# First output weights in a sixteen-place ring, and four kinds of load tied behind others, in a decoder trunk on one core

## The chip, the cores and the metric

The kernel runs on one core of one Trainium2 chip. The metric is the time of one execution in microseconds (us) of device time; lower is better. The engines are named as in the profile: PE is TensorE's matmul, PEld its weight load, DVE is VectorE, ACT is ScalarE, POOL is GpSimd, SP is SyncE. SP computes nothing here: it issues most of the DMA transfers, in its own program order, one after the other. A name with a q (SPq, ACTq) is that engine's sequencer, which issues DMAs. L1343 is line 1343 of the kernel before.

## The reference

One layer of a hybrid decoder (sequence 1024, model width 2048): two groups of eight heads, a projection of both, a gated embedding, two norms.

```python
hn = rmsnorm(h, norm_mix_g)
sb_q, sb_k, sb_v, sb_g, df_q, df_k, df_v, df_g = split(hn @ w_in)      # 2048 x 8192
sb_out = stick_breaking_attention(sb_q, sb_k, sb_v)                    # 8 heads of 128
df_out = differential_attention(rope(df_q), rope(df_k), df_v, lam)     # 8 heads, 2 x 64
df_out = rmsnorm(df_out, subln_g, 1e-5) * (1 - lambda_init)
mixed  = concat(sb_out * silu(sb_g), df_out * silu(df_g))
h = h + mixed @ w_out                                                  # 2048 x 2048
gate = sigmoid(rmsnorm(h, norm_ple_g) @ w_ple_gate)                    # 2048 x 2048
h = h + gate * (p @ w_ple_proj)                                        # 256 x 2048
return rmsnorm(h, norm_final_g)
```

All of it is float32.

## The kernel before

**Numbers.** Each float32 operand is split into a high and a low part (`hi`: a cast on ACT, `lo`: a subtraction on DVE), and a product is three matmuls, hi.hi, hi.lo and lo.hi. So each weight tile and each operand tile passes ACT and then DVE before PE can use it.

**Products by halves.** The sequence is cut into two halves of 512 columns. The three large products (value and gate columns of `w_in`; `w_out`; `w_ple_gate`) multiply 2 x 2 blocks with seven products instead of eight (`class Seven`). The seven are called A11, A12, S1, S2, S3, S4, A22; their operands are blocks or sums of blocks, kept in DRAM (`mixed_d`, `comb_d`, `h_d`, `hcomb_d`) and loaded back into SBUF (`load_operand`, `gate_operand`).

**Stages, in order of time.** Values and gates of all heads (to about 640 us), q and k projections with attention for the second half and then for the first half (`for half in (1, 0)`, 16 heads each, to about 1700 us), the output projection (`w_out`, to about 1980 us), the gate products with `w_ple_gate` (to about 2310 us), the end with the final norm.

**The first output products.** The products A11 and A12 of all eight units `u` of `w_out` (phase 0) run while the last head's attention still runs. Their split weights were made earlier and lie in DRAM (`wout_d[u, k, i]`: k is A11 or A12, i is hi or lo). `last_steps` hands their loads to `side`, a list of steps that are called after so many ticks; a tick is three matmuls of the main sequence. The last q/k unit is ticks 0 to 32, then come sixteen products of four ticks each in the order A11(0), A11(1), A12(0), A12(1), A11(2) and so on: A11(3) begins at tick 52. `weights_first(u, ...)` (L1338) loads two tiles of 512 KB for one u: one holds hi of A11 and of A12, the other lo of both. The tiles come from the places named by tag: `wraw`, `whi`, `wlo`, `st`, two places each. Unit 0 and unit 3 both take the two `wraw` places.

**Who sets the order.** The order on PE, ACT and DVE is that in which the code is written (`manual_schedule`). SP's and POOL's order is made by a scheduler with a simulated clock: a DMA is issued when, by that clock, its place and its data are free, however much later in the code it stands. On the chip SP then goes through that order strictly, and waits at each DMA until its place is really free. `tc.issue_after(x)` adds one condition to the scheduler: not ahead of x on that queue.

**The gate products.** `op.todo` lists the weight tiles in the order of use. `step()` is called after each half product (a slot: twelve matmuls): it casts the next weight tile on ACT (`whigh`, L758), subtracts on DVE (`wlow`, L772), calls what is due, and takes up to two entries from `xq`, which are splits of operands (L644 on ACT, L650 on DVE). Loads of the raw gate weights are `first_load` (L1545, for A11 and A12: `w_gate`), `second_load`, and `last_load` (L1563, for S3 and A22: from `tw_d`). `first_load` reuses one place for each product and half, so the load for unit u+1 waits until DVE is done with that of unit u. Only unit 7's A12 has a place of its own (`awl`).

`gate_loads` (L1266) calls `gate_operand` (L1250), which issues the DMA, and puts the split into `xq` to be taken `GLAT` slots later (3 for A11 and A12, 4 for S1, S2, S4, 2 for the others).

**The last pass** (second part of the gate stage: S3 and A22 of units 0 to 5, then 6 and 7 by column halves) needs for each unit u the residual tile `hpair[u]` (512 KB, `load_h`, L1982) for the addition at L2038, and for the second half's final scaling sixteen tiles `h_d[1, ch]` (256 KB, `final1`). Before, `load_h` is called for 0 to 3 ahead of the pass and for u+4 in unit u.

Of the kernel before, what the change touches and what calls it, by code (L numbers as in the profile page):

```python
# [13 lines left out]
F32 = mybir.dt.float32  # L14
F32R = mybir.dt.float32r
# [5 lines left out]
P = 128  # L21
# [14 lines left out]

PRIO = 300
GVT = 1, 2, 3, 4, 5, 6, 7, 8, 14, 15, 16, 17
GLAT = {'S4': 4, 'S1': 4, 'S2': 4}
TICK = {  # L40
    "sumlag": 2, "gvx": ((22, 27), (80, 85)), "chore": (36, 78, 87), "opx": (8, 12), "turn": 76, "lag": 15, "gap": (4, 6),
    "parts": (1, 2), "vparts": (3, 4), "sums": (0, 2), "squared": (3, 4.5), "norm": (1, 4),
# [9 lines left out]
    "begun": (86.5, 91.5, 93.5, 94.5, 93.5), "mid_turn": 76, "mid_lag": 17, "mid_gap": (4, 6),  # L52
    "mid_df_scores": (-20, -16, -9, -8.5, -1, -0.5, 4, 8), "mid_df_turn": (19, 17), "mid_df_v": -1, "mid_df_norm": 44.5,
    "mid_sb_scores": (-3, 5, 12.5, 21), "mid_sb_turn": (32, 36), "mid_sb_v": 22, "mid_taken": (28, 31),
# [15 lines left out]
def _body(ctx, nc, tc, ap):  # L70
# [3 lines left out]
    wp = ctx.enter_context(tc.tile_pool(name="wp", bufs=2))  # L74
# [174 lines left out]
    wout_d = dram.tile([8, 2, 2, P, HALF], F32R, name="wout_d", tag="wout_d")  # L249
# [30 lines left out]
    h_d = dram.tile([2, NK, P, HALF], F32, name="h_d", tag="h_d")  # L280
# [312 lines left out]
    with tc.tile_pool(name="at", bufs=2) as at, tc.tile_pool(name="pz", bufs=2, space=PSUM) as pz:  # L593
        SWAP = [i + 8 if i < 8 else i - 8 if i < 16 else i for i in range(32)]
        BUFS = {"cs": 1, "bt": 3}
# [498 lines left out]
        for ph in range(2):  # L1094
            for u in range(NVG):
# [3 lines left out]
                if ph:  # L1099
                    a = pp.tile([P, HALF], F32, name="pa", tag="acc", bufs=2)  # L1100
# [120 lines left out]


        op = Seven(lambda u, ph, k: ap["w_out"][u, ph, k], 8)
        tw_d = dram.tile([8, 2, P, 2, HALF], F32, name="tw_d", tag="tw_d")
        hcomb_d = dram.tile([4, 8, P, HALF], F32, name="hcomb_d", tag="hcomb_d")
        q_d = dram.tile([8, 2, P, HALF], F32, name="q_d", tag="q_d")
# [23 lines left out]
        def gate_operand(nm, i, eng):  # L1250

            hi, lo = op.places(GPLACE[nm][i], "g" + nm)
            src = {"A11": h_d[1, i], "A12": h_d[1, i + 8], "A22": h_d[0, i + 8]}.get(nm)
            if src is None:
                src = hcomb_d[SUMS.index(nm), i]
            gain = {"A11": i, "A12": i + 8, "A22": i + 8, "S3": i}.get(nm)
            if gain is not None:
                gain = gvec[:, 1, gain:gain + 1]
            if nm == "S3":
                with tc.issue_after(op.lastw.ins):  # L1260
                    eng.dma_start(lo.bitcast(F32), src)
            else:
                eng.dma_start(lo.bitcast(F32), src)
            return partial(op.split, "g" + nm, i, hi, lo, gain, apart=True)

        def gate_loads(nm, i0, n=4, eng=nc.sync):  # L1266
# [15 lines left out]
        kept, place = [], [0]  # L1282
# [52 lines left out]
                    side.add([(lag, load_operand(0, nm, i))])  # L1335
                side.add([(t0, load)])

        def weights_first(u, t0, pool, tags):  # L1338

            def load():  # L1340
                hl = [pool.tile([P, 2, 4 * P], F32R, name=f"wf{nm}", tag=t, bufs=2) for nm, t in zip(("hi", "lo"), tags)]
                for i in range(2):
                    nc.sync.dma_start(hl[i].bitcast(F32), wout_d[u, :, i].bitcast(F32).rearrange("k p n -> p k n"))  # L1343
                for k, nm in enumerate(("A11", "A12")):
                    op.wq[u, 0, nm] = hl[0][:, k], hl[1][:, k]

            side.add([(t0, load)])

        def last_steps():
            for nm in ("A11", "A12", "S2", "S4", "S1", "S3", "A22"):  # L1350
                operands(nm, *TICK[nm])
            raws, high = (wp, "wraw", "wraw"), (wp, "whi", "wlo")
            for u, (pool, *tags) in enumerate((raws, high, high, raws, high, high, (at, "st", "st"), high)):
                weights_first(u, TICK["wf"][u], pool, tags)
            side.add(zip(TICK["begun"], (begun, op.whigh, led, led, led)))

        def begun():
# [8 lines left out]
        cs = rope_of(1)  # L1366
# [4 lines left out]
        for half in (1, 0):  # L1371
            X = X0 if half == 0 else X1

            for hd in ORDER:
# [110 lines left out]
                q, k, qz, KL = qk[0], qk[1], qk.get("qz"), qk.get("kl")  # L1485
# [18 lines left out]
                if half == 1 and hd == ORDER[-2]:  # L1504
                    cs = rope_of(0)
# [32 lines left out]
        def wg(u, ks, b):  # L1538
            return ap["w_gate"][u, ks, b // 10 - 1][:, b % 10 - 1, :]

        raws = {}
# [3 lines left out]
        def first_load(u, nm, ks):  # L1545

            if u < 8:
                if u == 7 and nm == "A12":
                    t = at.tile([P, 4 * P], F32, name="wraw1", tag="awl")
                else:  # L1550
                    if (u, ks) == (0, 0):
                        first[nm] = wp.tile([P, 2, 4 * P], F32, name="wraw", tag="wraw", bufs=2)
                    t = first[nm][:, ks, :]
                raws.setdefault((u, nm), []).append(t)
                nc.sync.dma_start(t, wg(u, ks, 11 if nm == "A11" else 21))
            if ks and (u == 7 and nm == "A12" or u == 8 and nm == "A11"):
                first.pop(nm)
                w = wp.tile([P, 2, 4 * P], F32, name="wraw", tag="wraw", bufs=2)
                for i, b in enumerate((22, 21) if u == 7 else (12, 11)):
                    raws[0, 1, b] = w[:, i, :]  # L1560
                    second_load(0, 1, b)

        def last_load(u, nm):  # L1563
            if u < 8:
                w = wp.tile([P, 2, 4 * P], F32, name="wraw", tag="wraw", bufs=2)
                raws[u, nm] = [w[:, ks, :] for ks in range(2)]
                nc.sync.dma_start(w, tw_d[u, int(nm == "A22")])

        def second_load(u, ks, b):
            nc.sync.dma_start(raws[u % 2, ks, b], wg(u, ks, b))  # L1570
# [411 lines left out]
        def load_h(u):  # L1982
            if u < 8:
                hpair[u] = at.tile([P, 2, HALF], F32, name="h0", tag=HP[u], bufs=BUFS.get(HP[u], 2))
                nc.sync.dma_start(hpair[u], h_d[0].rearrange("(a k) p t -> k p a t", a=2)[u])

        def load_q(u):

# [6 lines left out]
        embedding(0)  # L1995
        plew(0, 1, "awl")
        plew(0, 0)
        for u in range(4):
            load_h(u)
        qs = {u: load_q(u) for u in range(3)}  # L2000
        s2 = ev.tile([P, HALF], F32, name="s2", tag="ssq")
# [14 lines left out]

        def final1(ch, u_):
            t = ftile()
            nc.sync.dma_start(t, h_d[1, ch])

            def fn():
                V.scalar_tensor_tensor(t, t, gvec[:, 2, ch:ch + 1], sums1[0], op0=ALU.mult, op1=ALU.mult)
                nc.sync.dma_start(out_f[ch * P:ch * P + P, Q:], t)

            if u_ < 5:
                op.soon.append((op.slot + 3, fn))
            else:
                late.append(fn)
# [44 lines left out]
        for u in range(6):  # L2073
            embedded = begin(u + 1) if u < 5 else None
            if u == 5:
                for c in (1, 0):
                    plew_load(7, c)
            gprod(u, "A22", bs[u], False)
            q1, _ = qs.pop(u)
            V.tensor_tensor(q1, bs[u], q1, op=ALU.add)  # L2080
            gating0(u, 0, q1, zs[u])
            if embedded:
                embedded()
            if u < 5:
                qs[u + 3] = load_q(u + 3)
            load_h(u + 4)
            if u == 0:
                sums1 = load_sums(1, ((ev, "rstd1", 1), (ev, "sq", 2)))
            elif u == 1:
                norm(sums1)  # L2090
            else:
                for ch in range(4 * u - 8, 4 * u - 4):
                    final1(ch, u)
# [265 lines left out]
```

## Time and profile before

| | |
|---|---|
| median of 3 runs | 2345.38 us (2342.2 to 2348.5) |
| profiled execution | 2351.75 us, span 2350.0 us |
| PE busy | 2315.6 us of the span (99%), 11089 matmuls |
| PEld, DVE, ACT, POOL busy | 82%, 76%, 54%, 13% |
| granted TensorE clock, mean | 0.996 |
| DMA | 556.66 MB, mean 237 GB/s |

The span runs from the first to the last instruction; the profiled execution's own time is 1.75 us more. Matmuls are pipelined: the record of a 128x512 one is about 0.39 us long, but in a full sequence one starts every 0.23 us, so the times that count are the starts. The idle time ahead of a matmul stands in brackets in the timeline, with what ended it.

### The profile page before, as it was taken

How to read it: one execution, taken by the hardware profiler on the slowest of the kernel's cores; microseconds unless marked ns; L12 is line 12 of the kernel's file. 1: busy time of each engine (PE TensorE's matmuls, PEld its weight loads, DVE VectorE, ACT ScalarE, POOL GpSimd, SP SyncE). 2: the span in 40 equal slices, each digit the busy share in tenths (PEclk: the TensorE clock that was granted, in tenths of full speed). 3: DMA queues.
4: the chain of work that ended last, by engine and by line, in shares of the span. 5: the costliest groups of instructions: out<-in, count | busy, mean ns of one | idle time of the engine just before them, and what ended most of it. 6: DMA issues, size and time to landing. Idle time of an engine off the chain costs nothing. (4 is left out here: it accounts for less than half of the span.)

```text
span 2350.0 us, 32639 instructions
## 1 busy us (share of the span) xinstructions
PE 2315.6 (99%) x11089; PEld 1931.3 (82%) x11089; DVE 1797.0 (76%) x3119; ACT 1268.5 (54%) x2303; POOL 296.2 (13%) x441
## 2 busy tenths in 40 slices
PE   9999999999999999999999999999899999999998
PEld 7878888888788888877888888888778887888777
DVE  7487776666578888877877878778677988687787
ACT  6323243333357776677766767677633435542455
POOL 2121111111100000000011010111021121111000
PEclk9999999999999999999999999999999999999999
DMA  8586788866787777787677667678798789998965
GB/s 268 204 293 229 254 276 229 209 157 131 210 266 258 238 252 258 254 288 253 199 201 203 181 198 216 194 206 255 221 246 203 248 245 286 308 349 258 336 210 185
DMA packets 255000, 556.66 MB, mean 237 GB/s; under 512 B 28512, under 2 KB 39008, under 8 KB 254832
## 3 DMA queue, kind: packets, MB, share of 16 engines
q1 hardware_dynamic: 185424, 395.92, 50.9%
q0 software_dynamic: 52848, 128.74, 22.5%
q10 hardware_dynamic: 16560, 29.92, 3.5%
q8 instruction: 87, 1.43, 0.2%
q14 instruction: 81, 0.66, 0.1%
HBM read 359.16 MB, written 203.69 MB: 240 GB/s over the span
## 5 line engine op out<-in xcount | busy, mean ns | idle before, releaser
L758 ACT CAST wpr<-T 128x512 fp32r<-128x512 f32 x208 | 127.1, 621 | 484.1 <-DVE T L717 406.4
L267 PE MATMUL acc<-xh,whi 128*128 128x512 f32 x768 | 313.1, 408 | 0.2 <-ACT whi L185 0.2
L269 PE MATMUL acc<-xh,wlo 128*128 128x512 f32 x768 | 301.6, 393 | 4.4 <-DMA wlo<-wlo_d 3.9
L268 PE MATMUL acc<-xl,whi 128*128 128x512 f32 x768 | 300.9, 392 | 0.0
L269 PEld LDWEIGHTS acc<-xh,wlo 128*128 128x128 f32 x768 | 144.4, 188 | 37.4 <-DMA wlo<-wlo_d 4.3
L267 PEld LDWEIGHTS acc<-xh,whi 128*128 128x128 f32 x768 | 144.9, 189 | 25.1 <-ACT whi L185 0.6
L268 PEld LDWEIGHTS acc<-xl,whi 128*128 128x128 f32 x768 | 145.1, 189 | 23.8 <-issue 0.2
L772 DVE TENSOR_TENSOR wpr<-T,wpr 128x512 fp32r<-128x512 f32 x208 | 142.4, 684 | 6.1 <-ACT wpr L758 3.0
L871 POOL DMA_DIRECT2D vg_d<-hc x128 | 89.1, 696 | 453.9 <-DVE hc L1089 263.1
L185 ACT CAST whi<-wraw 128x1024 fp32r<-128x1024 f32 x128 | 134.1, 1048 | 19.0 <-DMA wraw<-w_in 8.8
L758 ACT CAST wpr<-wraw 128x512 fp32r<-128x512 f32 x128 | 78.8, 617 | 106.3 <-DMA wraw<-tw_d 38.1
L406 ACT ACTIVATE et<-z,mx 128x512 f32<-128x512 f32 (+7 forms) x128 | 95.1, 743 | 60.6 <-DVE mx L398 60.6
L398 DVE CUSTOM_DVE_ANT_0 z<-z,wide 128x512 f32<-128x512 f32 (+7 forms) x128 | 97.5, 763 | 33.3 <-PE z L351 30.4
L477 DVE TENSOR_TENSOR awl<-tp,awh 128x256 fp32r<-128x256 f32 (+1 forms) x160 | 92.5, 578 | 34.9 <-ACT awh L472 33.9
L472 ACT CAST awh<-tp 128x256 fp32r<-128x256 f32 (+1 forms) x160 | 80.6, 504 | 51.4 <-PE tp L453 50.5
L772 DVE TENSOR_TENSOR wpr<-wraw,wpr 128x512 fp32r<-128x512 f32 x128 | 86.6, 684 | 17.2 <-ACT wpr L758 17.1
L381 DVE TENSOR_TENSOR_SCAN pt<-pt 128x511 f32<-128x511 f32 (+3 forms) x64 | 86.7, 1354 | 14.4 <-ACT pt L374 13.9
L181 DVE TENSOR_TENSOR wlo<-wraw,whi 128x1024 fp32r<-128x1024 f32 x56 | 68.5, 1223 | 15.3 <-ACT whi L185 14.8
L500 PE MATMUL av<-awl,v 128*128 128x256 f32 x256 | 72.9, 285 | 0.4 <-DVE awl L477 0.4
L498 PE MATMUL av<-awh,v 128*128 128x256 f32 x256 | 72.5, 283 | 0.5 <-ACT awh L472 0.4
L499 PE MATMUL av<-awh,v 128*128 128x256 f32 x256 | 72.4, 283 | 0.0
L413 ACT ACTIVATE et<-et,l 128x512 f32<-128x512 f32 (+3 forms) x64 | 49.4, 772 | 40.9 <-DVE l L412 40.9
(580 smaller groups left out, 6917.6 us busy)
## 6 DMA issues: line engine op xcount, KB each, us to landing
wraw<-w_in SPq DMA_DIRECT2D x128, 512.0 KB, 4.7
wlo<-wlo_d SPq DMA_DIRECT2D x72, 512.0 KB, 3.8
wraw<-w_vg SPq DMA_DIRECT2D x143, 256.0 KB, 3.6
vg_d<-hc POOLq DMA_DIRECT2D x128, 256.0 KB, 4.9
wlo_d<-wlo SPq DMA_DIRECT2D x56, 512.0 KB, 3.7
wraw<-w_gate SPq DMA_DIRECT2D x92, 256.0 KB, 5.3
h_d<-hc POOLq DMA_DIRECT2D x56, 256.0 KB, 5.1
wraw<-w_out SPq DMA_DIRECT2D x56, 256.0 KB, 4.5
```

The source lines that it names most:

```text
L185: side.later(1, lambda: A.copy(hi[:, o], raw[:, o]))
L267: T.matmul(acc[c], hi[:, k2, kh, c, :], xh, start=first, stop=False)
L268: T.matmul(acc[c], hi[:, k2, kh, c, :], xl, start=False, stop=False)
L269: T.matmul(acc[c], lo[:, k2, kh, c, :], xh, start=False, stop=last)
L381: V.tensor_tensor_scan(pt[:, w], pt[:, w], pt[:, w], initial=1.0, op0=ALU.mult, op1=ALU.bypass)
L398: V.tensor_tensor_reduce(z[:, vw], z[:, vw], add, -DF_SCALE, 3.0e38, ALU.add, ALU.min, mx)
L406: A.activation(et[:, vw], z[:, vw], AF.Exp, bias=mx[:, 0:1], scale=-1.0, accum_out=l[:, c:c + 1])
L472: A.copy(wh[:, o, :], tp[:, o, :])
L477: V.tensor_tensor(wl[:, o, :], tp[:, o, :], wh[:, o, :].bitcast(F32), op=ALU.subtract)
L758: A.copy(t[:, 0], src)
L772: V.tensor_tensor(t[:, 1], src, t[:, 0].bitcast(F32), op=ALU.subtract)
L871: G.dma_start(vg_d[hf, blk, u], o, **(dict(accum_op=ALU.add) if ph else {}))
```

## The change

Five edits.

1. `weights_first` loads one tile for each product (u, k), with hi and lo of that product, in one DMA of 512 KB; sixteen DMAs, as before. The tiles go round a longer ring: `wraw`, `wraw`, `cs`, `whi`, `wlo`, `whi`, `wlo`, twice, and `st` for the last two. The times of the requests are sixteen instead of eight.
2. The DMAs of the gate operands A12, blocks 0 to 3, are issued after the last `first_load` that stands ahead of them in the code (`op.lastf`).
3. The gate weights A12 of unit 7 are issued after the last of the other `first_load`s (`op.lastf`).
4. `load_h` is called for units 0 and 1 ahead of the last pass, behind the load of gate operand A22 block 3 (`op.lasta[0]`), and for u+2 in unit u, behind the last `tw_d` load (`op.lastl`). The loads of `final1` also go behind `op.lastl`.
5. The splits of the gate operands S3 are taken one slot later (`GLAT` 3 instead of 2).

```diff
-GLAT = {'S4': 4, 'S1': 4, 'S2': 4}
+GLAT = {'S4': 4, 'S1': 4, 'S2': 4, 'S3': 3}
...
-    "wf": (21.5, 25, 33, 45, 49, 61, 65.5, 77),
+    "wf": (18, 21.5, 22, 25, 25.5, 33, 33.5, 38, 42, 46, 50, 54, 58, 62, 66, 70),
...
-            if nm == "S3":
-                with tc.issue_after(op.lastw.ins):
+            if nm == "S3" or nm == "A12" and i < 4:
+                with tc.issue_after((op.lastw if nm == "S3" else op.lastf).ins):
                     eng.dma_start(lo.bitcast(F32), src)
             else:
-                eng.dma_start(lo.bitcast(F32), src)
+                op.lasta[i // 4] = eng.dma_start(lo.bitcast(F32), src)
...
-        def weights_first(u, t0, pool, tags):
+        def weights_first(u, k, t0, pool, tag):
             def load():
-                hl = [pool.tile([P, 2, 4 * P], F32R, name=f"wf{nm}", tag=t, bufs=2) for nm, t in zip(("hi", "lo"), tags)]
-                for i in range(2):
-                    nc.sync.dma_start(hl[i].bitcast(F32), wout_d[u, :, i].bitcast(F32).rearrange("k p n -> p k n"))
-                for k, nm in enumerate(("A11", "A12")):
-                    op.wq[u, 0, nm] = hl[0][:, k], hl[1][:, k]
+                t = pool.tile([P, 2, 4 * P], F32R, name="wfhl", tag=tag, bufs=BUFS.get(tag, 2))
+                nc.sync.dma_start(t.bitcast(F32), wout_d[u, k].bitcast(F32).rearrange("i p n -> p i n"))
+                op.wq[u, 0, ("A11", "A12")[k]] = t[:, 0], t[:, 1]
...
-            raws, high = (wp, "wraw", "wraw"), (wp, "whi", "wlo")
-            for u, (pool, *tags) in enumerate((raws, high, high, raws, high, high, (at, "st", "st"), high)):
-                weights_first(u, TICK["wf"][u], pool, tags)
+            raw, high, low, st, cs_ = (wp, "wraw"), (wp, "whi"), (wp, "wlo"), (at, "st"), (at, "cs")
+            ring = raw, raw, cs_, high, low, high, low, raw, raw, cs_, high, low, high, low, st, st
+            first_of = [(u + i, k) for u in range(0, 8, 2) for k in range(2) for i in range(2)]
+            for (u, k), t0, place in zip(first_of, TICK["wf"], ring):
+                weights_first(u, k, t0, *place)
...
-                nc.sync.dma_start(t, wg(u, ks, 11 if nm == "A11" else 21))
+                if u == 7 and nm == "A12":
+                    with tc.issue_after(op.lastf.ins):
+                        nc.sync.dma_start(t, wg(u, ks, 21))
+                else:
+                    op.lastf = nc.sync.dma_start(t, wg(u, ks, 11 if nm == "A11" else 21))
...
-                nc.sync.dma_start(w, tw_d[u, int(nm == "A22")])
+                op.lastl = nc.sync.dma_start(w, tw_d[u, int(nm == "A22")])
...
-                nc.sync.dma_start(hpair[u], h_d[0].rearrange("(a k) p t -> k p a t", a=2)[u])
+                with tc.issue_after((op.lasta[0] if u < 2 else op.lastl).ins):
+                    nc.sync.dma_start(hpair[u], h_d[0].rearrange("(a k) p t -> k p a t", a=2)[u])
...
-        for u in range(4):
+        for u in range(2):
             load_h(u)
...
-            nc.sync.dma_start(t, h_d[1, ch])
+            with tc.issue_after(op.lastl.ins):
+                nc.sync.dma_start(t, h_d[1, ch])
...
-            load_h(u + 4)
+            load_h(u + 2)
```

More of the change, by code (lines that the diff above doesn't have):

```diff
@@ L1223, in _body @@
         op = Seven(lambda u, ph, k: ap["w_out"][u, ph, k], 8)
+        op.lasta = [None, None]
         tw_d = dram.tile([8, 2, P, 2, HALF], F32, name="tw_d", tag="tw_d")
```

2 rows, old and new, of the table TICK are left out of this document.

## The prediction, made before the changed kernel was run

> **What bounds the kernel now.** I read the profile in this order: busy time by engine, the waits of PE, the timeline of PE around its longest waits, the timeline of SP for the DMAs behind them, and a table of stretches for clock, DMA and DVE.
>
> ```profile
> PE 2315.6 (99%) x11089; PEld 1931.3 (82%) x11089; DVE 1797.0 (76%) x3119; ACT 1268.5 (54%) x2303; POOL 296.2 (13%) x441
> PE pa L665 <- DMA wflo<-wout_d: 3.0, 1, 3.0
> PE pa L663 <- DMA wfhi<-wout_d: 2.3, 1, 2.3
> PE pa L1790 <- ACT s L1856: 1.9, 1, 1.9
> PE pb L1790 <- DVE qt L2080: 1.2, 1, 1.2
> PE pb L1790 <- DVE qt L2057: 1.1, 1, 1.1
> PE z L1703 <- DVE pl L1681: 0.5, 1, 0.5
> PE z L1704 <- DVE pwhl L1695: 0.4, 1, 0.4
> ```
>
> PE is busy for 99% of the span, and the change takes no matmul away. So it can only win PE's waits, and what a wait costs after it. The columns of the waits are the sum in us, how often, and the longest. The first two are one place, a first output product that waits for its weights. The third is the start of the gate stage. The last four lie in the last pass: 1.2 + 1.1 + 0.5 + 0.4 = 3.2 us.
>
> **The change part by part.**
>
> *The ring of the first output weights.* The timeline of PE around the first two waits (start, record length, instruction, idle time ahead of it):
>
> ```profile
> 1642.50 0.39 PE L663 MATMUL pa<-cA11h,wfhi 128*128 128x512 f32 x1
> 1645.72 0.39 PE L664 MATMUL pa<-cA11l,wfhi 128*128 128x512 f32 x1
> 1646.64 0.40 PE L665 MATMUL pa<-cA11h,wflo 128*128 128x512 f32 x1
> 1649.37 0.47 PE L663 MATMUL pa<-cA11h,wfhi 128*128 128x512 f32 x1 [2.33 <-DMA wfhi<-wout_d]
> 1653.07 0.79 PE L665 MATMUL pa<-cA11h,wflo 128*128 128x512 f32 x1 [3.00 <-DMA wflo<-wout_d]
> 1658.55 0.40 PE L664 MATMUL pa<-cA11l,wfhi 128*128 128x512 f32 x1
> ```
>
> 1642.50 is the first matmul of A11 of unit 2, 1649.37 that of unit 3. It should have started 0.23 us after 1646.64, at 1646.87. From the first matmul of a product to the second of its second block (L664), with the attention's matmuls between, unit 2 took 1645.72 - 1642.50 = 3.22 us. Unit 3 has one short attention matmul more between (0.12 us), so it would have come to 1646.87 + 3.34 = 1650.21, and came at 1658.55: 8.3 us lost. Of that 5.3 us is idle time; the other 3.0 us is slow running after it, which the stretches show (length, busy us with instruction counts of PE, PEld, DVE, ACT, POOL, granted clock, DMA share, GB/s):
>
> ```profile
> 1630.00:1640.00 10.00, 10.00 (x56) 8.61 (x55) 9.31 (x18) 6.87 (x14) 3.10 (x4) 1.00 0.84 294
> 1640.00:1650.00 10.00, 7.67 (x40) 5.89 (x37) 7.01 (x16) 5.40 (x12) 1.74 (x3) 1.00 1.08 262
> 1650.00:1660.00 10.00, 7.00 (x27) 6.00 (x27) 2.20 (x6) 1.46 (x4) 0.00 (x0) 0.66 0.89 287
> ```
>
> The granted clock falls to 0.66 in the ten microseconds after the wait began: the wait is followed by half speed. The Trainium skill, page "TensorE: Matmul & The Clock Gate", Part 1, has PE drop to half rate after about one idle window of 3.4 us and return after one busy window of that length. By that page one window at half rate would cost 1.7 us (an estimate), and this place 5.3 + 1.7 = 7.0 us instead of 8.3. The trace has 3.0 us, and I go by the trace.
>
> Why the weights were late:
>
> ```profile
> 1639.03 0.86 SPq L1343 DMA_DIRECT2D wfhi<-wout_d  x1
> 1639.98 1.56 SPq L1343 DMA_DIRECT2D wflo<-wout_d  x1
> DMA to landing us min/median/max: 4.5/5.7/13.0
> ```
>
> Unit 3 takes both `wraw` places of unit 0, and they are free when A12 of unit 0 ends (tick 44). SP issues at 1639.03 and 1639.98, and the second lands about 13 us later, the longest of the eight, with the DMA engines full (1.08). It was needed eight ticks after the place was free.
>
> In the new ring I go through all sixteen places. A11 of unit 3 is in `whi`, whose place is free when the last q/k unit ends (tick 32), and is needed at tick 52. From the eighth tile on, each takes the place of a product six or more places before: `wraw` is free at ticks 36 and 40 for products at 60 and 64, `cs` at 44 for 68, `whi` and `wlo` at 48 to 60 for 72 to 84. All have 20 ticks or more from a free place to the need. From 1625 on, where the last unit ends, a tick is more than a microsecond (eight ticks took from about 1639 to 1647), so 20 ticks are over 20 us, against 13.0 us for the slowest landing. The first three come in places that are free inside the last unit. Bytes and number of DMAs stay the same (sixteen of 512 KB). The price of the wait, 8.3 us, should go.
>
> What is late next: DVE. It was busy for 9.31 of 10 us just ahead of the wait and only 2.20 in the ten after, so the wait gave it time to catch up; without it the attention's steps follow more closely. PE ran with that DVE load without a stop from 1630 to 1640, so I charge only 0.8 us, between 0 and 4 us (half the prize).
>
> SP gets other waits in its order: each new load waits for the end of one product instead of two. What stands behind it can be late by at most one product, four ticks, some 4 us, and the loads behind (operands of the next products, `w_out` blocks) are needed tens of ticks later. The two `w_out` blocks that go into the second `wraw` place start up to 4 ticks later, for a cast at tick 91.5. I cost that at nothing; the cover is the 23 ticks between.
>
> *A12 operands and unit 7's gate weights.* Start of the gate stage, SP and ACT:
>
> ```profile
> 1953.95 1.03 SPq L1555 DMA_DIRECT2D wraw<-w_gate  x2
> 1956.62 3.26 SPq L1555 DMA_DIRECT2D wraw<-w_gate  x4
> 1965.05 2.95 SPq L1263 DMA_DIRECT2D cgA12l<-h_d  x4
> 1968.34 0.33 SPq L1555 DMA_DIRECT2D wraw<-w_gate  x1
> 1971.06 0.62 ACT L758 CAST wpr<-wraw 128x512 fp32r<-128x512 f32 x1 [1.30 <-DMA wraw<-w_gate]
> 1976.85 0.62 ACT L758 CAST wpr<-wraw 128x512 fp32r<-128x512 f32 x1 [1.75 <-DMA wraw<-w_gate]
> 1981.30 0.63 ACT L1289 ACTIVATE rsq<-hc 128x512 f32<-128x512 f32 x1 [1.56 <-DMA sq_d<-rsq]
> ```
>
> Two and four `w_gate` loads go out ahead of any cast. Units 0 and 1 share four places, so six must hold the two of unit 7, which are not cast until 28 weight tiles later. The change sends them away. The four A12 operands of 1965.05 (1 MB) move behind the second load of unit 1's A11, which is the one of 1968.34: it lands with 1 MB less ahead of it, and ACT's 1.75 us at 1976.85 should shrink. Whether PE's 1.9 us goes depends on the wait at 1981.30, since between it and the copy that PE waits for ACT has no pause. That is a DMA of squares in the same full queues. The operands themselves now land later, about 1976 to 1979 by 6 to 8 us from 1969 to 1971, and ACT takes the first two at 1977.9 or sooner. So the gain lies between 1.9 us and a loss of about 1 us. I take 1.2.
>
> *The last pass.*
>
> ```profile
> 2205.00:2210.00 5.00, 5.00 (x22) 3.72 (x20) 4.96 (x9) 2.97 (x6) 0.00 (x0) 1.00 1.06 392
> 2260.00:2280.00 20.00, 20.00 (x90) 16.57 (x89) 15.45 (x26) 11.81 (x20) 0.00 (x0) 1.00 0.36 119
> 2197.87 3.11 SPq L1985 DMA_DIRECT2D h<-h_d  x4
> 2205.83 0.40 SPq L1567 DMA_DIRECT2D wraw<-tw_d  x1
> 2211.59 1.97 SPq L1985 DMA_DIRECT2D h<-h_d  x4
> h<-h_d SPq DMA_DIRECT2D x8, 512.0 KB, 10.1
> wraw<-tw_d SPq DMA_DIRECT2D x16, 512.0 KB, 3.9
> 2214.34 0.62 ACT L758 CAST wpr<-wraw 128x512 fp32r<-128x512 f32 x1 [6.37 <-DMA wraw<-tw_d]
> 2217.27 0.39 PE L1790 MATMUL pb<-cgS3h,wpr 128*128 128x512 f32 x1
> 2230.30 0.72 ACT L644 ACTIVATE cgA22h<-cgA22l,gvec 128x512 fp32r<-128x512 f32 x1 [1.61 <-DMA cgA22l<-h_d]
> 2242.29 0.38 SPq L1567 DMA_DIRECT2D wraw<-tw_d  x1
> 2260.38 0.69 DVE L2038 TENSOR_TENSOR h<-h,qt 128x512 f32<-128x512 f32 x1
> ```
>
> All eight residual tiles (4 MB) go out at 2197.87 to 2213.6, in the stretch where the DMA engines are full (1.06). The weights issued at 2205.83 land 8.5 us later instead of their median 3.9, and ACT waits 6.37 us for them; A22's operands are late too. From there the lateness goes through ACT and DVE to PE's four waits. The change moves six of the eight tiles (3 MB, some 8 us of DMA time at 392 GB/s) past 2240, into a stretch where the share falls to 0.36. PE's 3.2 us is the most that can be won. I take 2.8.
>
> Are they in time? The tile of unit 2 goes behind the `tw_d` load of 2242.29 and is first used by the addition at 2260.38: 18 us, against 10.1 us for the landing in the full queues. Each later one has the same distance, one unit, some 13 us after the last. The loads of `final1` are used three slots after they are asked for; they leave the full stretch too.
>
> The later S3 splits frame a small risk: the last pair now stands behind the cast of 2214.34 on ACT. The row leaves 2.9 us (2214.34 to 2217.27, where PE starts S3) for cast, norm and split, too little if that weight tile lands as late as before. With the residual tiles gone it should land about 4 us sooner. Between 0 and 3 us; I take 0.
>
> *Sum.* 8.3 - 0.8 + 1.2 + 2.8 = 11.5 us. Against the profiled execution's own 2351.75 us (span 2350.0 and 1.75 around it) that is 2340.2 us. The median of the runs shown is 2345.38, 6.4 us below the profiled one, and I take the same gain from it: 2333.9 us.
>
> **The rivals.**
>
> *Only the ring wins.* The gate stage and the last pass keep their waits, or the S3 splits give back what the residual tiles win: 8.3 - 0.8 = 7.5 us, 2337.9 us. For it: the 1.9 us hangs on the squares' DMA, which no edit moves. Against it: the full DMA share exactly where the loads are taken out.
>
> *The ring's prize is given back.* The attention of the last head is bound by DVE, so that PE waits in small pieces for what it waited for in one: half of 8.3 and all other gains gone, 4 us, 2341.4 us. For it: 9.31 of 10 us. Against it: no stop of PE in that stretch. That a load is simply not asked earlier is excluded by the places in the code.
>
> *The residual tiles come late (slower).* Each is now behind a weight load that itself waits for DVE, and DVE's addition holds up all behind it on DVE, the additions that free PE's accumulators too. The margin is 18 - 10 = 8 us. If a tile lands later than 18 us after its turn, DVE stands in each of six units. To be slower by 0.3% (7 us) this must take back 11.5 + 7 us, about 3 us a unit: landings 21 us after the turn, twice the 10.1. Then 2353 us. The Trainium skill, page "DMA: Bandwidth & Descriptors", section on rules for kernel authors, speaks for this rival: issue a DMA early and wait on it late. The trace's rows speak against it here, since early is when the queues were full.
>
> *More than forecast.* A late weight tile costs this at the start of the output stage:
>
> ```profile
> 1731.84 0.50 PE L663 MATMUL pbc<-cS2h,wpr 128*128 128x512 f32 x1 [1.21 <-ACT wpr L758]
> ```
>
> If SP's new order happens to bring that tile's load forward, the 1.21 us and a spell at half clock like the one above (3 us) go as well: 2329.7 us.
>
> **How the numbers follow.** About 0.3%, 7 us, is what a measurement of this kernel can tell from no change. Forecast 0.46; only the ring 0.21; given back 0.14; slower 0.10; more 0.09. Faster by over 7 us (below 2338.3): forecast, more, and half of the ring's case, whose 2337.9 is at the bound: 0.66. Same: the other half and the given-back case less a little: 0.22. Slower: 0.12, the residual tiles and unforeseen waits from SP's reordering. The predicted time is 2333.9. The range goes down to 2328 (the case of more, with 2 us of run spread) and up to 2347 (the given-back case with its spread, up to the time before).
>
> **What would show it.** Right: no wait of PE on a load from `wout_d`, and a granted clock of 1.00 between 1640 and 1660; a `tw_d` landing near 4 us and no ACT wait above 3 us around 2205; residual loads spread past 2240; PE's third wait below 1 us. Wrong: DVE additions at L2038 waiting for `h<-h_d`, PE waits for attention tiles after 1640, or new waits on `w_out` blocks behind SP.

## The result, and the profile after

The changed kernel takes 2334.32 us (median of 4 runs, 2332.48 to 2337.18), the kernel before, run beside it, 2346.34 us: a ratio of 0.9952, 95% interval 0.9933 to 0.9971, so 12.0 us less. A second comparison (in the last experiment below) gave 2336.27 against 2345.22 us, 0.9968 (0.9955 to 0.9980), 9.0 us less. Ratios and intervals come from all fast runs and not from the two medians; one slow run of the kernel before (4141.65 us, at a granted clock of 0.718) is left out of them in the second comparison. In us, the two intervals are 6.8 to 15.7 and 4.7 to 10.6. The forecast was 11.5 us less, 2333.9 us: inside the first interval and just above the second.

The page of the changed kernel, its span and its busy times:

```profile
span 2334.0 us, 32642 instructions
PE 2310.0 (99%) x11089; PEld 1928.0 (83%) x11089; DVE 1796.7 (77%) x3119; ACT 1269.0 (54%) x2303; POOL 296.7 (13%) x441
```

The waits of PE (sum in us, how often, the longest), the four largest:

```profile
PE acc L269 <- DMA wlo<-wlo_d: 3.0, 1, 3.0
PE pbc L665 <- DVE wpr L772: 1.8, 4, 0.7
PE av L495 <- DVE lead L476: 1.3, 1, 1.3
PE ple L1707 <- DVE qt L2044: 1.2, 1, 1.2
```

No wait on a load from `wout_d` is left, and none of the four of the last pass. The first of these four waits lies near 1057 us, far ahead of every edit, and was 3.9 us in the profile before. The fourth is new. (Line numbers are a few higher than before: L1795 here is L1790 there, L1572 is L1567.) The stretches around the old wait on the first output weights (length, busy us with instruction counts of PE, PEld, DVE, ACT, POOL, granted clock, DMA share, GB/s):

```profile
1630.00:1640.00 10.00, 10.00 (x54) 8.50 (x53) 9.31 (x17) 6.38 (x14) 3.51 (x5) 1.00 1.08 377
1640.00:1650.00 10.00, 10.00 (x56) 8.56 (x55) 8.07 (x19) 6.42 (x14) 1.33 (x2) 1.00 1.07 273
1650.00:1660.00 10.00, 10.00 (x57) 8.56 (x56) 6.96 (x12) 8.95 (x17) 0.83 (x1) 1.00 1.05 391
```

The clock stays at 1.00, and DVE, no longer idle in the third stretch, keeps up.

The two profiled executions differ by 15.9 us (2351.75 and 2335.83), more than the medians. To see which of it belongs to the edits, I cut the time of PE by the starts of seven matmuls that every kernel has: the first one after 1040 us, the first output product, S2 of the output stage (first one on `cS2h`), A11 of the gate stage, S3 of the last pass, the first quarter product (`pbq`), and the last matmul. The columns are the differences. All profiles of this study, in us (the kernels are told of below; E1 to E5 are the edits):

| kernel | to first output product | first output products | output stage | gate, to S3 | last pass | end |
|---|---|---|---|---|---|---|
| before | 585.37 | 79.29 | 268.92 | 243.64 | 86.92 | 37.01 |
| changed | 584.47 | 70.88 | 266.45 | 241.51 | 82.50 | 38.94 |
| E1 alone | 584.22 | 70.92 | 268.42 | 243.11 | 85.05 | 37.01 |
| without E1 | 584.38 | 78.11 | 267.78 | 242.33 | 82.50 | 38.07 |
| short ring | 582.78 | 70.89 | 267.04 | 243.26 | 82.50 | 38.30 |
| without E4 | 583.40 | 70.90 | 267.24 | 242.89 | 88.80 | 37.02 |
| without E5 | 584.30 | 70.94 | 266.73 | 242.40 | 82.50 | 37.95 |
| without E2, E3 | 587.06 | 70.89 | 268.97 | 242.26 | 82.50 | 38.63 |
| the same, fewer squares | 584.87 | 70.90 | 264.92 | 241.43 | 82.50 | 37.09 |
| changed, end mended | 584.65 | 70.90 | 270.20 | 243.03 | 82.50 | 37.01 |
| changed, again | 582.99 | 70.90 | 265.37 | 243.82 | 82.50 | 37.51 |
| three orders | 584.26 | 70.91 | 264.68 | 243.11 | 82.50 | 37.02 |
| four orders | 581.83 | 70.88 | 264.45 | 241.46 | 82.50 | 37.01 |
| four orders, again | 583.34 | 70.91 | 264.88 | 242.02 | 82.50 | 37.01 |

Two columns hardly move except with an edit: the first output products (70.9 us with the new ring, 78 to 79 without) and the last pass (82.50 us with edit 4 in every profile, 85 to 89 without). Three columns vary by 2 to 5 us between kernels that are alike there. So of the profiled pair's difference 8.4 us (first output products) and 4.4 less 1.9 us (last pass, end) belong to the edits, 10.9 us; the other 5.5 us (0.9 + 2.5 + 2.1) lie in columns that vary by themselves. (Both make 16.4 us; 0.5 us of it goes again ahead of 1040 us and behind the last matmul.)

### The profile page after: what moved, and what is told of

Same layout as the page of the kernel before. It is cut to its first block, busy times and chain, and to the rows that moved or that the text cites. A ratio compares the mean times of both kernels' runs of the same rounds, so it can differ in the third digit from the quotient of the medians.

```text
span 2334.0 us, 32642 instructions
## 1 busy us (share of the span) xinstructions
PE 2310.0 (99%) x11089; PEld 1928.0 (83%) x11089; DVE 1796.7 (77%) x3119; ACT 1269.0 (54%) x2303; POOL 296.7 (13%) x441
## 5 line engine op out<-in xcount | busy, mean ns | idle before, releaser
L758 ACT CAST wpr<-wraw 128x512 fp32r<-128x512 f32 x128 | 78.8, 617 | 110.2 <-DMA wraw<-tw_d 37.1
```

The lines of the kernel that those rows point to most:

```text
L758: A.copy(t[:, 0], src)
```

## The experiments

**The ring alone, and all but the ring.** The first is the kernel before with the new `weights_first`, its sixteen times and its ring; the second is the changed kernel with the same lines the other way round.

```diff
-    "wf": (21.5, 25, 33, 45, 49, 61, 65.5, 77),
+    "wf": (18, 21.5, 22, 25, 25.5, 33, 33.5, 38, 42, 46, 50, 54, 58, 62, 66, 70),
...
-                hl = [pool.tile([P, 2, 4 * P], F32R, name=f"wf{nm}", tag=t, bufs=2) for nm, t in zip(("hi", "lo"), tags)]
+                t = pool.tile([P, 2, 4 * P], F32R, name="wfhl", tag=tag, bufs=BUFS.get(tag, 2))
...
-            for u, (pool, *tags) in enumerate((raws, high, high, raws, high, high, (at, "st", "st"), high)):
-                weights_first(u, TICK["wf"][u], pool, tags)
+            ring = raw, raw, cs_, high, low, high, low, raw, raw, cs_, high, low, high, low, st, st
+            for (u, k), t0, place in zip(first_of, TICK["wf"], ring):
+                weights_first(u, k, t0, *place)
```

> The kernel before with edit 1 alone (one tile for each first output product, ring of sixteen places). Theory of separate waits: the stage of the first output products gains the 8.4 us that the two profiles show, and the start of the output stage 2.5 us more, because its 1.21 us wait on a late weight tile and the spell at half clock behind it go when PE and DVE reach it without the long wait before; so 10 to 11 us under the kernel before, about 2335.4, and the waits of the gate stage (1.9 us) and of the last pass (3.2 us) stay as they were. My prediction's own sum for this edit was 7.5 us, 2338.8. Rival, the ring is everything: as fast as the changed kernel, 12 us under the kernel before.

> The changed kernel with edit 1 undone (eight pairs of first output weight tiles as before; edits 2 to 5 stay). Separate waits: the 5.3 us wait on the first output weights is back with two half-clock windows, and the 1.21 us wait in the output stage with one, while the gate stage keeps 2.1 us and the last pass 2.5 us (4.4 less 1.9 at its end): 4.6 us under the kernel before, about 2341.7. Rival, only the ring wins: the same as the kernel before, 2346. Rival, the output stage's 2.5 us does not come from the ring: that wait stays away here too, about 2339.

The ring alone took 2338.01 us against 2346.23, 0.9965 (0.9953 to 0.9978): 8.2 us less, near my prediction's 7.5 and below the 10 to 11 that I expected. Without the ring it was 2343.26 us, 0.9987 (0.9978 to 0.9996): 3.0 us less. The ring is most of the gain. How much isn't settled by the times: 8.2 us are two thirds of the first comparison's 12.0 and nine tenths of the second's 9.0. That it isn't all rests on the kernel without it, whose interval ends below 1, and on the last pass, which is 85.05 us with the ring alone and 82.50 without the ring. PE around the first output products without the ring, with the stretch after it:

```profile
1647.62 0.47 PE L663 MATMUL pa<-cA11h,wfhi 128*128 128x512 f32 x1 [1.42 <-DMA wfhi<-wout_d]
1651.09 0.79 PE L665 MATMUL pa<-cA11h,wflo 128*128 128x512 f32 x1 [2.76 <-DMA wflo<-wout_d]
```

```profile
1650.00:1660.00 10.00, 8.91 (x41) 7.84 (x41) 2.20 (x6) 3.38 (x6) 0.00 (x0) 0.67 0.97 332
```

The wait is back in the same place, 4.2 us this time instead of 5.3, again with a clock of 0.67 behind it. The output stage did not follow the ring: with the ring alone PE waited 2.04 us for a weight tile near 1723 us, so the 2.5 us that the changed kernel's profile shows there are no by-product of it.

**Is it the finer tiles or the longer ring?** One tile for each product, with the sixteen request times, but only in the eight places of before:

```diff
-            ring = raw, raw, cs_, high, low, high, low, raw, raw, cs_, high, low, high, low, st, st
+            ring = raw, high, raw, low, high, raw, low, raw, high, low, high, low, st, high, st, low
```

> The changed kernel with the ring cut back to the eight places of before (wraw, whi, wlo, st; no cs, and no run of seven before a place comes round), still one tile for each product. If what counts is that a place is given back after one product instead of two, every tile's place is still free 12 ticks or more ahead of its need, so no wait on a load from wout_d, 70.9 us from the first output product to S2, and the changed kernel's time within 1 us (2334). If the longer ring is what counts, the wait on these loads comes back in part: 72 to 79 us in that stretch and up to 8 us more, 2335 to 2342.

2336.22 us against 2346.42, 0.9954 (0.9942 to 0.9966), and 70.89 us in the stretch, with no wait on `wout_d`. One tile for each product, so that a place comes back after one product instead of two, is enough; the two extra places buy nothing that shows here. What the new request times and the new order of the places alone would do was not taken apart from the tiles. (The time is 2 us above what I expected, but it is that of the changed kernel in the second comparison, 2336.27.)

**The last pass.** First edit 4 undone (residual tiles and `final1` as before), edit 5 kept; then edit 5 undone and edit 4 kept.

```diff
-                with tc.issue_after((op.lasta[0] if u < 2 else op.lastl).ins):
-                    nc.sync.dma_start(hpair[u], h_d[0].rearrange("(a k) p t -> k p a t", a=2)[u])
+                nc.sync.dma_start(hpair[u], h_d[0].rearrange("(a k) p t -> k p a t", a=2)[u])
...
-        for u in range(2):
+        for u in range(4):
             load_h(u)
...
-            with tc.issue_after(op.lastl.ins):
-                nc.sync.dma_start(t, h_d[1, ch])
+            nc.sync.dma_start(t, h_d[1, ch])
...
-            load_h(u + 2)
+            load_h(u + 4)
```

```diff
-GLAT = {'S4': 4, 'S1': 4, 'S2': 4, 'S3': 3}
+GLAT = {'S4': 4, 'S1': 4, 'S2': 4}
```

> The changed kernel with edit 4 undone (all residual tiles asked for as before, final1's loads free). Separate waits: the four waits of the last pass (3.2 us) and ACT's wait of over 5 us on a weight load near the residual loads are back, and the 1.2 us wait of PE near the end, which is new in the changed kernel, goes: 4.4 lost and 1.9 regained, 2.5 us above the changed kernel, about 2336.8. Rival, the new wait near the end has nothing to do with the moved residual loads: it stays, and the whole 4.4 us is lost, about 2338.7. Rival, the last pass gains by the later S3 splits: no waits come back.

> The changed kernel with edit 5 undone (S3 operands split two slots after their request, as before). If the residual tiles alone won the last pass, the stretch from S3 to the quarters stays at 82.5 us and the time within 1 us of the changed kernel's 2334.3. If the later split is needed with them, PE waits for A22's or S3's splits and the stretch is 84 us or more, 2336 or more.

Without edit 4: 2340.99 us against 2346.23, 0.9978 (0.9970 to 0.9987), 5.2 us less instead of 12.0 or 9.0, and 4.2 us above what I expected. Its last pass is 6.3 us longer than the changed kernel's, where I expected 4.4. SP, ACT and PE in its last pass:

```profile
2197.52 2.04 SPq L1990 DMA_DIRECT2D h<-h_d  x4
2200.27 0.62 ACT L758 CAST wpr<-wraw 128x512 fp32r<-128x512 f32 x1 [5.36 <-DMA wraw<-tw_d]
2206.99 0.50 PE L1796 MATMUL pb<-cgS3l,wpr 128*128 128x512 f32 x1 [0.81 <-DVE cgS3l L650]
2225.39 0.50 PE L1795 MATMUL pb<-cgA22h,wpr 128*128 128x512 f32 x1 [1.99 <-ACT cgA22h L644]
2226.88 0.50 PE L1796 MATMUL pb<-cgA22l,wpr 128*128 128x512 f32 x1 [1.00 <-DVE cgA22l L650]
```

With the residual tiles early again, ACT waits 5.36 us for a weight tile, and PE waits for splits of S3 and of A22: 88.80 us, more than the 85 to 87 with edits 4 and 5 both out, though one profile of each doesn't settle that difference. The wait for `cgS3l` is the risk that I had named for edit 5. Without edit 5 the last pass stays at 82.50 us, and the kernel took 2336.20 us, 0.9958 (0.9946 to 0.9970): edit 5 does nothing that shows. The new loss in the last column goes with edit 4: 37.1 to 38.9 us with it, 37.0 without, as long as nothing else is mended there.

**The start of the gate stage.** Edits 2 and 3 undone, and then this kernel with the last transfers of squares left out, so that the norm lacks these squares:

```diff
-            if nm == "S3" or nm == "A12" and i < 4:
-                with tc.issue_after((op.lastw if nm == "S3" else op.lastf).ins):
+            if nm == "S3":
+                with tc.issue_after(op.lastw.ins):
...
-                if u == 7 and nm == "A12":
-                    with tc.issue_after(op.lastf.ins):
-                        nc.sync.dma_start(t, wg(u, ks, 21))
-                else:
+                if True:
                     op.lastf = nc.sync.dma_start(t, wg(u, ks, 11 if nm == "A11" else 21))
```

```diff
                 V.tensor_tensor(t, t, t0, op=ALU.add)
-                add_squares(2 * hf, t)
+                if nsq[2 * hf] < 5:
+                    add_squares(2 * hf, t)
```

> The changed kernel with edits 2 and 3 undone (A12 operands and unit 7's gate weights asked for as before). Separate waits: PE's wait of about 1.9 us at the start of the gate stage is back, ACT waits again 1.5 us or more on a gate weight load there, 2.1 us above the changed kernel, about 2336.4; the first output products and the last pass stay as in the changed kernel. Rival: that wait hung on the squares' transfer and on the lead that PE has, not on these loads, and the time is the changed kernel's within 0.5 us.

> The kernel without edits 2 and 3 (A12 operands and unit 7's gate weights early), and without the last three transfers of squares of each half into sq_d, so that the norm lacks these squares. In the six profiles PE's wait at the start of the gate stage is the time from the first gate product to the last squares on ACT less 5.8 us, and these squares wait for the place that such a transfer reads. If that transfer sets the wait, it is gone here, and the stretch from the first gate product to S3 is about 241.5 us, although edits 2 and 3 are out. If the gate weights and A12 operands set it, PE still waits 0.5 to 1.9 us there, and the stretch is 242.3 us or more.

Without edits 2 and 3: 2337.66 us, 0.9965 (0.9952 to 0.9979), and a wait of PE of 0.50 us there. Over all profiles that keep the order of the squares, the wait is 0, 0.59, 0.65, 1.12, 1.26, 1.50 and 2.07 us with edits 2 and 3, and 0.50, 1.35 and 1.89 without. They don't decide it. What does is on ACT. From top to bottom the changed kernel, the same kernel in its second profile, and the kernel without the squares' transfers:

```profile
1964.52 0.62 ACT L758 CAST wpr<-wraw 128x512 fp32r<-128x512 f32 x1 [0.84 <-DMA wraw<-w_gate]
1967.56 0.63 ACT L1290 ACTIVATE rsq<-hc 128x512 f32<-128x512 f32 x1 [2.42 <-DMA sq_d<-rsq]
1972.21 0.56 ACT L1861 COPY s<-pa 128x512 f32<-128x512 f32 x1
```

```profile
1967.32 0.63 ACT L1290 ACTIVATE rsq<-hc 128x512 f32<-128x512 f32 x1 [1.96 <-DMA sq_d<-rsq]
1971.97 0.56 ACT L1861 COPY s<-pa 128x512 f32<-128x512 f32 x1
1972.58 0.50 PE L1795 MATMUL pa<-cgA12h,wpr 128*128 128x512 f32 x1 [2.07 <-ACT s L1861]
```

```profile
1963.64 0.63 ACT L1290 ACTIVATE rsq<-hc 128x512 f32<-128x512 f32 x1
1968.29 0.57 ACT L1859 COPY s<-pa 128x512 f32<-128x512 f32 x1
```

The copy `s<-pa` comes 4.65 us after the squares in all three, and where PE waits (the second), it waits for the copy. The squares wait for a transfer into `sq_d`, which still reads the place they write to. In the kernel before the wait for the weight tile ahead of it was 1.75 us and that for the transfer 1.56; in the changed kernel it is 0.84 and 2.42. Edits 2 and 3 did bring the weights earlier, and the transfer took what they won. With the last transfers left out, PE doesn't wait, and the column is 241.43 us, although edits 2 and 3 are out (2333.08 us of two runs, 0.9944, 0.9926 to 0.9961). This kernel also moves less data. But with three orders, below, the transfers stay, these squares stand behind the copy, and PE's wait is gone as well. So the squares, held up by the transfer, set this wait, and edits 2 and 3 are worth nothing that can be seen.

**The new wait near the end.** SP, ACT, DVE and PE of the changed kernel:

```profile
2281.86 2.15 SPq L2026 DMA_DIRECT2D hc<-h_d  x4
2284.11 0.38 SPq L1572 DMA_DIRECT2D wraw<-tw_d  x1
2290.65 1.15 ACT L758 CAST wpr<-wraw 128x512 fp32r<-128x512 f32 x2 [8.37 <-DMA wraw<-tw_d]
2292.51 2.73 DVE L2029 SCALAR_TENSOR_TENSOR hc<-hc,gvec,sums 128x512 f32<-128x512 f32 x4
2295.17 0.68 DVE L2044 TENSOR_TENSOR qt<-qt,ple 128x512 f32<-128x512 f32 x1
2295.90 0.50 PE L1707 MATMUL ple<-ph,pwhl 128*128 128x512 f32 x1 [1.22 <-DVE qt L2044]
```

The last weight tile is asked for behind four loads of `final1`, and ACT starts on it 6.5 us later; DVE, late by it, does four scalings before the product that PE waits for. The experiment asks for these four loads one slot later and leaves their use where it was:

```diff
-                op.soon.append((op.slot + 3, fn))
+                op.soon.append((op.slot + 3 - (u_ == 4), fn))
...
-                for ch in range(4 * u - 8, 4 * u - 4):
-                    final1(ch, u)
+                def finals(u=u):
+                    for ch in range(4 * u - 8, 4 * u - 4):
+                        final1(ch, u)
+
+                if u == 4:
+                    op.soon.append((op.slot + 1, finals))
+                else:
+                    finals()
```

> The changed kernel with one thing more: the four loads of final1 in unit 4 are asked for one slot later, so that the last tw_d load goes ahead of them on SP. If these four loads (1 MB) delay the last weight tile and so cause the 1.2 us wait of PE near the end, that wait goes, the last stretch is 37.0 us as before instead of 38.1 to 38.9, and the time about 1.5 us below the changed kernel's: 2332.8. If the delay comes from the moved residual tiles or from when the tile's place is free, the last stretch stays at 38 to 39 us and the time at 2334.3.

SP and ACT there:

```profile
2287.23 0.33 SPq L1572 DMA_DIRECT2D wraw<-tw_d  x1
2287.65 1.81 SPq L2026 DMA_DIRECT2D hc<-h_d  x4
2290.48 1.14 ACT L758 CAST wpr<-wraw 128x512 fp32r<-128x512 f32 x2 [2.79 <-DMA wraw<-tw_d]
```

ACT starts on the tile 3.3 us after its request, the wait is gone, and the end is 37.01 us, as expected. The time, 2335.19 us, 0.9955 (0.9943 to 0.9967), does not show 1.5 us: the interval is wider than that, and this profile has a longer output stage than any other.

**The waits that vary.** What is left sits in columns where the edits don't show. In the output stage SP stands at a load from `comb_d` with the next `w_out` loads behind it, in the changed kernel for 4.4 us (SP's own waits from 1705 to 1716 us); near 1057 us SP stands at loads of x with a `wlo` load behind them (changed kernel):

```profile
SPq L1238 <- DMA comb_d<-sg: 4.4, 1, 4.4
```

```profile
1050.83 3.09 SPq L1211 DMA_DIRECT2D xl<-h_d  x4
1054.01 0.45 SPq L187 DMA_DIRECT2D wlo<-wlo_d  x1
```

Two kernels change these orders. The first has the mended end, puts the last row's squares behind the copy that PE waits for, and ties the second phase's operand loads behind the last `w_out` load; the second also issues the sixteen loads of x from POOL:

```diff
-            eng.dma_start(lo.bitcast(F32), src)
+            if ph and eng is nc.sync:
+                with tc.issue_after(op.lastw.ins):
+                    eng.dma_start(lo.bitcast(F32), src)
+            else:
+                eng.dma_start(lo.bitcast(F32), src)
...
-                op.soon.append((op.slot + 2, partial(row_squares, hf, o)))
+                op.soon.append((op.slot + (3 if (hf, ch) == (1, 15) else 2), partial(row_squares, hf, o)))
...
-            nc.sync.dma_start(lo.bitcast(F32), h_d[0, kt])
+            G.dma_start(lo.bitcast(F32), h_d[0, kt])
```

> The changed kernel with three orders changed, after the waits that the runs left: final1's four loads of unit 4 one slot later (as before); the loads of the second phase's output operands on SP tied behind the last w_out load, so that SP no longer stands for 4 to 5 us at a load from comb_d with w_out loads behind it; the last row's squares one slot later on ACT, behind the copy that PE waits for at the start of the gate stage. If these three are what sets the waits: no wait of PE on a weight tile near 1723, 265 us from S2 to the first gate product (266.5 to 269 so far); no wait near 1975, 241.5 us from there to S3 (242 to 243.6 where it waited); 37.0 us for the last stretch; together about 3.5 us below the changed kernel, 2331. Rival: the output stage's weight tile waits for its own place and not behind SP's load, and the operands' loads, now later, make PE wait where the second phase begins: 266.5 us or more, 2333 to 2336.

> The same, and the sixteen loads of x for the second q/k half are issued by POOL instead of SP. In the profiles SP stands at these loads for 10 us and more around 1040 to 1065 with loads of wlo behind them, and PE waits 0.3 to 4.5 us for a wlo tile near 1057. If SP's order sets that wait, it goes, and the stretch from 1040 to the first output product is 582 us or less (582.8 to 587.1 so far): 2 to 3 us below the kernel with three orders changed, about 2328.5. If the full DMA queues set it, the wait stays at 1 to 3 us and the time is that of the other.

Three orders: 2332.69 us against 2345.54, 0.9941 (0.9927 to 0.9954). Four: 2332.57 us, 0.9936 (0.9923 to 0.9948). All the aimed-at waits are gone. Three orders came out 1.7 us above what I expected, four orders 4 us. With four orders PE's largest waits are these, and SP near 1057 goes straight to its `wlo` loads:

```profile
PE av L495 <- DVE lead L476: 1.3, 1, 1.3
PE warm L876 <- POOL eps L93: 1.0, 1, 1.0
```

```profile
1046.53 0.32 SPq L187 DMA_DIRECT2D wlo<-wlo_d  x1
1049.58 0.33 SPq L193 DMA_DIRECT2D wraw<-w_in  x1
1054.33 0.32 SPq L187 DMA_DIRECT2D wlo<-wlo_d  x1
```

The stretch from 1040 to 1070 us (columns as above), first of the changed kernel, then with four orders:

```profile
1040.00:1070.00 30.00, 27.00 (x126) 22.19 (x125) 23.21 (x43) 23.67 (x45) 1.96 (x3) 0.94 0.91 303
```

```profile
1040.00:1070.00 30.00, 27.85 (x134) 22.19 (x133) 24.58 (x48) 26.04 (x50) 9.23 (x17) 1.00 0.99 357
```

The DMA share is higher without the wait (0.99) than with it (0.91). That speaks for SP's order and against full queues, but doesn't settle it: of the twelve profiles with the old order, one (without E4) has no wait there either. The gain is small in any case. Where this wait is gone, PE waits 0.84 to 1.45 us for ACT some 9 us later; the column, which I expected at 582 us or less, is 581.83 and 583.34 us, against 582.78 to 587.06 with the old order; and four orders take the time of three.

The output stage is 264.4 to 264.9 us in all three profiles with the new order, against 265.4 to 270.2 in the ten of kernels with all squares and the old order. SP's order isn't all that counts there: the kernel with fewer squares has 264.92 us and no wait for that tile, though SP stands at `comb_d` for 4.1 us in it. The gate column is 243.11 us with three orders, though its first wait is gone; two small waits in it make 0.6 us, and the rest I can't name.

**The changed kernel and four orders side by side.** Both once more, on one chip:

> The changed kernel itself, timed beside the kernel with four orders changed on the same chip: 12 us under the kernel before, 0.9945 to 0.9955 of its time, and in the profile 70.9 us, 82.5 us and 38 to 39 us in the stretches that the edits touch.

> The kernel with four orders changed, again: none of the waits at 1020 to 1058, 1707 to 1725, 1975 and 2296, and 4 us or more below the changed kernel in the median, if what the four waits cost in the changed kernel (0 to 3 us each with what follows) is more than the spread of the runs; within 2 us of it if the runs shown so far were lucky.

The changed kernel took 2336.27 us against 2345.22, 0.9968 (0.9955 to 0.9980), so 9.0 us and not 12 us less, and its end was 37.51 us and not 38 to 39; four orders took 2331.35 us, 0.9940 (0.9928 to 0.9953). That is 4.9 us below the changed kernel, and its runs (2329.49 to 2332.88) all lie below all of the other's (2334.16 to 2341.63). It beats both kernels.

## Why the prediction was right

The time came out 0.4 us from the forecast in the first comparison and 2.4 us in the second, inside the range both times. But some terms of the sum were off, and they made up for each other; that the total came so close is in part luck.

- *Ring, 8.3 us.* Right: 79.29 to 70.88 is 8.4 us, the idle time and the slow running behind it. That the price varies I didn't say; the kernel without edit 1 paid 7.2 us (78.11 less 70.9).
- *Given back through DVE, 0.8 us.* Wrong, nothing: 70.88 to 70.94 us in all twelve profiles with one tile per product. DVE was busy 9.31 of 10 us ahead of the place as before, and PE did not wait.
- *SP's waits and the later `w_out` blocks, 0.* Nothing that shows: PE's wait for a `w_out` tile some 27 us into the output stage is between nothing and 2.04 us in the profiles with the ring, and 0.79 and 1.21 us in the two without.
- *A12 operands and unit 7's weights, 1.2 us.* Failed. The condition that I stated, that it "depends on the wait at 1981.30", decided it: that wait, for the squares' transfer, grew by what the weight's wait lost. I took 1.2 of 1.9 to -1 us and should have taken 0.
- *Residual tiles, 2.8 of 3.2 us.* Right in mechanism; the size is open. I summed PE's listed waits; the stretch shortened by 4.4 us, and by 2.6 us from the 85.05 of the ring alone, which had shorter waits there. The `tw_d` loads did not come back to 4 us (median 4.7, against 3.9 before), and ACT still waits over 3 us for some of them, but PE no longer waits for what follows.
- *`final1` behind `op.lastl`, 0.* Failed: edit 4 costs 0.1 to 1.9 us at the end. Of these loads I had only asked whether they would be in time, not what would stand behind them: the last weight tile did.
- *S3 splits later, 0.* Right with edit 4; its risk showed only without it.

By the columns that the edits move, that is 8.4 + 4.4 - 1.9 = 10.9 us from the one pair of profiles, where I had 11.5.

The rivals: "only the ring" was 2337.9, and the ring alone measures 2338.01, so it was well priced, but the last pass does win by its column. "Given back" and "residual tiles late" did not happen; in the last pass DVE waits for ACT and PE only, never for `h<-h_d`. The Trainium skill, page "DMA: Bandwidth & Descriptors", section "Rules for kernel authors", advises to issue a DMA early and wait for it late. Here it was the other way round: asking for the residual tiles early cost 2.6 to 6.3 us in the last pass. "More than forecast" seemed true in the first profile, where the wait near 1731 was gone, but SP's order around that tile had not changed: PE waited there 2.04 us with the ring alone and 1.85 us with the end mended.

## What to carry to other kernels

Give a buffer back after the smallest unit of work that uses it: one tile per product in the old places, asked for one by one, removed the whole wait. Keep loads that are needed late out of a stretch where the queues are full, but look at which urgent load the moved ones then stand ahead of. And before a difference of two profiles is put down to an edit, compare the same stretches in several profiles: here a third of the pair's difference lay in places that differ by as much between kernels that are alike there.

## What was not expected of the hardware

Whether a short wait of PE is followed by half speed is not decided by its length. Two kernels at the same place of the output stage, first the ring alone, then the changed kernel with the end mended; for each the matmul with its wait, and two stretches from 1722 us:

```profile
1723.55 0.50 PE L663 MATMUL pbc<-cS2h,wpr 128*128 128x512 f32 x1 [2.04 <-ACT wpr L758]
```

```profile
1722.00:1728.00 6.00, 4.03 (x16) 3.02 (x17) 5.93 (x11) 2.39 (x4) 1.38 (x2) 1.00 0.57 118
1728.00:1734.00 6.00, 6.00 (x28) 4.95 (x28) 5.34 (x9) 2.45 (x5) 1.17 (x2) 1.00 1.01 328
```

```profile
1724.08 0.50 PE L663 MATMUL pbc<-cS2h,wpr 128*128 128x512 f32 x1 [1.85 <-ACT wpr L758]
```

```profile
1722.00:1728.00 6.00, 3.73 (x12) 2.50 (x11) 5.93 (x10) 2.39 (x4) 0.84 (x1) 0.85 0.48 102
1728.00:1734.00 6.00, 6.00 (x24) 4.86 (x23) 3.98 (x7) 0.62 (x1) 1.68 (x2) 0.87 1.04 327
```

In both kernels a second wait, of 0.42 us, follows soon after, so the sum of the two doesn't decide either. The longer wait kept the clock at 1.00; after the shorter one it fell to 0.85 and 0.87, as means over 6 us. Its output stage is 1.8 us longer (270.20 against 268.42), though the wait was shorter. In the kernel before, 1.21 us at this place was followed by a fall too, to 0.72:

```profile
1732.00:1738.00 6.00, 5.58 (x17) 4.12 (x18) 4.87 (x9) 1.56 (x3) 1.70 (x2) 0.72 0.71 187
```

The Trainium skill, page "TensorE: Matmul & The Clock Gate", Part 1, says that the window by which PE's activity is judged runs freely, which fits that the length doesn't decide; that it takes one idle window of about 3.4 us does not fit, since 1.21 and 1.85 us were enough here. It may be one reason why the runs of one kernel spread by some 7 us (2341.78 to 2349.22 for the kernel before); that was not tested.
